# Gate loads in pieces and a different pace of gathers in a two-layer decoder trunk on one Trainium2 core

## The chip, the cores and the metric

The kernel runs on one core of one Trainium2 chip. The metric is the device time of one execution in microseconds (us); lower is better. Times given as "before" are the median of three timed runs, with the lowest and the highest. The profile is one further execution, with a time of its own. Engines are called as in the profile: PE (matrix engine), DVE (vector), ACT (scalar), POOL (GpSimd) and SP (which here only issues DMAs).

## What is computed

A decoder trunk of two layers for 512 tokens of width 1024, in float32. Each layer has a mixer (layer 1: gated linear attention and memory attention; layer 2: stick-breaking attention and memory attention), a layer norm, and then PEER: a feed-forward layer that picks, for each token and each of 8 heads, 16 of 16384 experts, and a second layer norm. Only PEER is touched by the change:

```python
def apply_experts(args):            # xt (128, D), it and gt (128, heads, 16): indices and gates
    xt, it, gt = args
    act = jax.nn.gelu(jnp.einsum('nd,nhkd->nhk', xt, u_tab[it]), approximate=False)
    return jnp.einsum('nhk,nhkd->nd', gt * act, v_tab[it])
...
h = layer_norm(DEEPNORM_ALPHA * h + mix, ln_g[layer, 0], ln_b[layer, 0])
ffn = peer(h, peer_w_q[layer], peer_subkeys[layer], peer_u[layer], peer_v[layer])
h = layer_norm(DEEPNORM_ALPHA * h + ffn, ln_g[layer, 1], ln_b[layer, 1])
```

## The kernel before, in words

`peer` runs twice (called "the first PEER" and "the second PEER" here). It treats the 512 tokens in two ways.

*Dense, for 384 tokens.* All 16384 experts are computed for these tokens, 128 experts at a time, in `P` = 128 blocks. A first pass, **u** (`ublock`), multiplies a block of `u_tab` with the tokens and keeps the gelu of it (`act`, written to `Ad` in DRAM, or `keep` in SBUF for the last 16 blocks). Each float32 operand is split in a high and a low part (`split`: `uh`, `ul` or `vh`, `vl`), and a product takes three matmuls: high by high, high by low, low by high (lines 117 to 119 in u, 289 to 293 and 1866 to 1868 in v). Meanwhile the top 16 of the scores are found, and turned into a dense table of gates, which goes to `Gd` in DRAM. A second pass, **v** (`vprep` and the loop behind it), reads the gates back (`gl`), multiplies them with the activations (`w`, line 1798), splits that (`whi` on ACT, line 1809, `wlo` on DVE, line 1810), and multiplies it with a block of `v_tab` into accumulators that stay in PSUM for the whole pass. v takes the 16 blocks in `keep` first (for the first 6 of them the gates lie in the tile named `keep` too), then the other 112. In v one block is 18 matmuls of 512 columns: 3 token tiles by two halves of the width by three.

*Gathered, for 128 tokens, and u of 32 more.* POOL fetches one expert row per token by an indirect DMA (`gather`, line 1167, a tile `gr` of 128x1024, `PF` = 3 ahead), and DVE takes a product with it: `gather_u` in a dot product with the tokens (a SCALAR_TENSOR_TENSOR at line 1109, written `gr<-gr,xnat`), `gather_v` in a sum (`va`, line 1246). A PEER has 160 gathers of u (128 and two times 16) and 128 of v, 288 together. They are put between the dense blocks by the `Stream` `gus`: each block hands it a budget in nanoseconds, each gather costs 1200 of it, and what is left is carried over. The budget is `GQ` in the query part ahead of u, `GU` in u while the selection (`work`) goes on, `GU2` after that up to block `KB` = 112, `GU3` for blocks 112 to 126, and in v `vb`, which is computed so that the gathers end `VE` blocks ahead of v's end. When the 128 gathers of v are done, `finish(0, ...)` takes the layer norm of their 128 tokens on DVE (`lny`, line 1022, to `xnat`, line 1039).

*Order.* In `peer` the order on PE, DVE, ACT and POOL is that of the code. In v, `vprep(b + 2)` stands ahead of the matmuls of block b, so a block is prepared two blocks before it is multiplied; the last `TAIL` = 6 blocks are prepared ahead and multiplied at the end, one token tile after another. The order on SP's queue is set by the framework's scheduler. The rows of `u_tab` and `v_tab` (512 KB a block, `ur` and `vr`, line 82) have `RB` = 4 buffers: the load of block i waits on SP until `vl` of block i-4 is done, and what stands behind it on SP waits too.

*Gate loads before.* v's gates come in nine loads: one for the first 6 blocks (into `keep`), one for the next 10 (tag `gx`), and seven for 16 blocks each (3072 KB, tags `big` and `xhl` by turns). The second and the third are issued on ACT's queue by `preload(1)` and `preload(2)`, the others on SP's by `vprep`, one DMA each. The activations `al` (352 KB for two blocks) are loaded on SP too.

```python
if b < P - 1:
    gus(GU if work.q else GU2 if b < KB else GU3)
...
vb = 1200 * (2 * P + SD - gcount[0] + PF) / (P - VE - VS)
```

Of the kernel before, what the change touches and what calls it, by code (L numbers as in the profile page):

```python
# [1066 lines left out]
NSUB = TD // TS  # L1067
AB = 2
AL = 2
GB = 16  # L1070
GA = 6
OT = 4
DT = 8
WB, WB0 = 900, 1850
GU = 1200
WP = 1100
LOG = 0
PF = 3
VS = 3
GD = 1  # L1080
G0 = 6
VE = 8
GU2 = 1850
GU3 = 1850
WF = 6100
ER = 6
GQ = 900
# [26 lines left out]
def peer(E, mixer, wq, sk, ut, vt, un, lng, lnb, out_dram=None, follow=()):  # L1114


    nc, tc = E.nc, E.tc
    Gd = E.dram.tile([NSUB, P, P, TS], F32, tag="Gd", name="Gd")
# [7 lines left out]
    with ExitStack() as pp:  # L1126
# [129 lines left out]
        with ExitStack() as up:  # L1256
# [449 lines left out]
            def ublock(b):  # L1706
# [28 lines left out]
                if b < P - 1:  # L1735
                    gus(GU if work.q else GU2 if b < KB else GU3)
                if LOG:
# [18 lines left out]
        gcuts = [0, G0] + list(range(KEEP, P + 1, GB))  # L1756
        vorder = list(range(KB, P)) + list(range(KB))

        def new_gates(i, i1):
            k = gcuts.index(i)  # L1760
            pool, tag = (wv, "gx") if k == 1 else (gp, "big") if k % 2 else (E.xp, "xhl")
            return pool.tile([P, NSUB, i1 - i, TS], F32, tag=tag, name="gl", bufs=1)

        def load_gates(eng, dst, b, b1):
            eng.dma_start(dst, Gd[:, :, b:b1].rearrange("s p i n -> p s i n"))

        pre = {}

        def preload(k, eng=nc.scalar):
            i, i1 = gcuts[k:k + 2]  # L1770
            pre[i] = new_gates(i, i1)
            load_gates(eng, pre[i], vorder[i], vorder[i] + i1 - i)

        def vprep(i):
            if i >= P:
                return
            b = vorder[i]
            raw = load_raw(E, vt[b * P:(b + 1) * P], "vr")
            if i + GA in gcuts[3:-1]:
                preload(gcuts.index(i + GA), nc.sync)  # L1780
            if i in gcuts:
                if i == 0:
                    vp["g"] = g0
                    load_gates(nc.sync, g0, b, b + G0)
                else:
                    vp["g"] = pre.pop(i)
                vp["i"] = i
            if b >= KB:
                av = keep[:, b - KB]
            else:  # L1790
                if b % AL == 0:
                    vp["a"] = wv.tile([P, AL, TU], F32, tag="al", name="al", bufs=3)
                    nc.sync.dma_start(vp["a"].rearrange("p (g a) n -> p g a n", a=AB), Ad[b // AB:b // AB + AL // AB].rearrange("g p a n -> p g a n"))
                av = vp["a"][:, b % AL]
            w = wv.tile([P, TD], F32, tag="w", name="w")
            whi = wv.tile([P, TD], F32R, tag="whi", name="whi", bufs=TAIL)
            wlo = wv.tile([P, TD], F32R, tag="wlo", name="wlo", bufs=TAIL)
            nc.vector.tensor_mul(w[:, :TU].rearrange("p (s n) -> p s n", n=TS), vp["g"][:, :TU // TS, i - vp["i"]],  # L1798
                                 av.rearrange("p (s n) -> p s n", n=TS))
            nc.scalar.activation(w[:, TU:].rearrange("p (s n) -> p s n", n=TS), vp["g"][:, TU // TS:, i - vp["i"]], AF.Copy)  # L1800
            pool, j = None, i - (P - TAIL)
            if j == 0:
                vp["tb"] = gp.tile([P, 16 * NT * P], F32R, tag="big", name="vtail")
            if 0 <= j < 4:
                pool = lambda name: vp["tb"][:, (2 * j + "hl".index(name[-1])) * D:][:, :D]
            elif j >= 4:
                pool = lambda name: gp.tile([P, D], F32R, tag="gr", name=name, bufs=PF + 1)
            hi, lo = split(E, raw, "v", pool)
            nc.scalar.activation(whi, w, AF.Copy)  # L1809
            nc.vector.tensor_sub(wlo, w, whi.bitcast(F32))  # L1810
            vp[i] = (whi, wlo, hi, lo)

        tail = []
        with written:
# [4 lines left out]
            acc = [[psum(E, name=f"acc{t}_{h}") for h in range(2)] for t in range(ND)]  # L1819
            vb = 1200 * (2 * P + SD - gcount[0] + PF) / (P - VE - VS)  # L1820

            preload(1)
            for b in range(P):
                vprep(b + 2)
                if b == 6:
                    preload(2)
                if b >= P - TAIL:
                    tail.append(vp.pop(b))
                    continue
                whi, wlo, hi, lo = vp.pop(b)  # L1830
                for t in range(ND):
                    sl = slice(t * P, (t + 1) * P)
                    mov_mm(E, acc[t], whi[:, sl], wlo[:, sl], hi, lo, b == 0, False)
                if b == P // 2:
                    vp["ln"] = load_ln(E, wv, lng, lnb)
                if b == P // 2 + 8:
                    warm_sqrt(E, vp["ln"][0])
                if b >= VS:
                    gus(vb)
# [14 lines left out]
            for t in range(ND):  # L1854
                sl = slice(t * P, (t + 1) * P)
# [4 lines left out]
                else:  # L1860
                    c = 0
                    for a in parts:
                        hs = slice(c, c + a.shape[-1])
                        c = hs.stop
# [99 lines left out]
```

## Time and profile before

| | |
|---|---|
| three timed runs | median 2860.54 us, lowest 2859.91, highest 2874.1 |
| the profiled execution | 2854.29 us, its span 2852.5 us |
| DVE busy | 2398.5 us (84%) |
| ACT busy | 1440.2 us (50%) |
| POOL busy | 969.8 us (34%) |
| moved by DMA | 821.25 MB, mean 288 GB/s |
| chain that ended last | PE 67%, DVE 12%, DMA 8%, issue 7%, POOL 4%, ACT 2% |
| the two dense passes, from the trace | u from 331 to 881 us and 1748 to 2299 us, v from 886 to about 1425 us and 2303 to about 2845 us |

The span goes from the first to the last instruction on the profile's clock; the profiled execution's own time is 1.8 us longer. A row of waits reads: engine, tile and line that waited, then `<-` what released it, then total us, number of times, and the longest one. A row of the timeline reads: start, duration, engine (with a q: its queue), line, operation, tiles out`<-`in, shapes, and in brackets the idle time before it with what ended that. A row of windows gives the stretch, its length, busy us of each engine with the instructions in it, the clock that TensorE was granted (1.00 is full), the busy share of the 16 DMA engines, and GB/s. GB/s rows of the DMA view divide their window into 40 equal slices.

### The profile page before, as it was taken

To read this page: it belongs to the slowest core of one execution; us is meant where nothing else is said; L and a number is where in the kernel's file an instruction comes from. 1 tells how busy PE (TensorE), PEld (TensorE's weight loads), DVE (VectorE), ACT (ScalarE), POOL (GpSimd) and SP (SyncE) were. 2 spreads that over 40 slices of the span, in tenths; PEclk is the share of its full clock that TensorE was granted. 3 is DMA by queue.
4 is the path that set the end of the run, shared out by engine and by line. 5 is a ranking of instruction groups with operands and counts; after the bars stand their busy time and mean duration, and the time that the engine had idled before them with its cause. 6 is when DMAs were issued, how large, how long until landed. Compare 5 with 4: busy or idle time off the path is not lost.

```text
span 2852.5 us, 44767 instructions
## 1 busy us (share of the span) xinstructions
PE 2806.3 (98%) x16235; PEld 2479.6 (87%) x16235; DVE 2398.5 (84%) x4806; ACT 1440.2 (50%) x2699; POOL 969.8 (34%) x675
## 2 busy tenths in 40 slices
PE   9999999999999999999999999999999999999998
PEld 8888999999998888788787889999999988887886
DVE  5565999999887888788968859999998878887888
ACT  6342447668683334333346434475786733333432
POOL 0102534343343344344100025344433524443440
PEclk9999999999999999999999999999999999999999
DMA  5332599999999999999621326999999999999994
GB/s 195 111 104 78 183 309 337 323 339 349 368 402 350 367 365 376 364 359 364 214 71 48 111 89 208 321 329 319 345 358 373 389 355 359 365 368 360 371 365 156
DMA packets 274701, 821.25 MB, mean 288 GB/s; under 512 B 34384, under 2 KB 83760, under 8 KB 268080
## 3 DMA queue, kind: packets, MB, share of 16 engines
q1 hardware_dynamic: 154880, 411.09, 40.6%
q0 software_dynamic: 82944, 302.03, 29.3%
q10 hardware_dynamic: 36656, 105.28, 9.6%
q8 instruction: 127, 2.08, 0.3%
q14 instruction: 94, 0.77, 0.1%
HBM read 723.31 MB, written 92.90 MB: 286 GB/s over the span
## 4 chain that ended last, share of the span: by engine, by line
PE 67%; DVE 12%; DMA 8%; issue 7%; POOL 4%; ACT 2%; ACTq 0%; POOLq 0%; DVEq 0%; SPq 0%
PE acc L291 9%; PE acc L289 9%; PE acc L293 9%; DMA vr<-in_vt 7%; PE ph L117 5%; PE ph L119 5%; PE ph L118 5%; POOL gr L1167 4%; DVE gr L1109 3%; PE pq L117 2%; PE pq L118 2%; PE pq L119 2%; DVE ul L1109 2%; PE bsp L117 1%; PE pss L1666 1%
## 5 line engine op out<-in xcount | busy, mean ns | idle before, releaser
L117 PE MATMUL ph<-xhl,uh 128*128 128x352 f32 x2048 | 674.6, 329 | 0.0
L119 PE MATMUL ph<-xhl,ul 128*128 128x352 f32 x2048 | 662.5, 323 | 5.6 <-DVE ul L1109 5.2
L118 PE MATMUL ph<-xhl,uh 128*128 128x352 f32 x2048 | 660.7, 323 | 0.0
L1167 POOL DMA_INDIRECT gr<-in_vt,gidx x256 | 376.7, 1471 | 526.4 <-DVE va L1246 465.6
L1167 POOL DMA_INDIRECT gr<-in_un,gidx x256 | 336.9, 1316 | 541.6 <-DVE gr L1109 446.8
L289 PE MATMUL acc<-vh,whi 128*128 128x512 f32 x1480 | 460.6, 393 | 22.2 <-ACT whi L1809 22.2
L97 ACT ACTIVATE vh<-vr 128x1024 fp32r<-128x1024 f32 x248 | 262.2, 1057 | 396.6 <-PE acc L293 270.7
L291 PE MATMUL acc<-vl,whi 128*128 128x512 f32 x1480 | 460.3, 392 | 1.0
L293 PE MATMUL acc<-vh,wlo 128*128 128x512 f32 x1480 | 458.5, 391 | 0.0
L98 DVE TENSOR_TENSOR vl<-vr,vh 128x1024 fp32r<-128x1024 f32 x248 | 303.1, 1222 | 165.2 <-ACT vh L97 164.8
L97 ACT ACTIVATE uh<-ur 128x1024 fp32r<-128x1024 f32 x288 | 303.8, 1055 | 227.1 <-PE ph L118 163.1
L119 PEld LDWEIGHTS ph<-xhl,ul 128*128 128x128 f32 x2048 | 385.1, 188 | 10.1 <-DVE ul L1109 8.7
L118 PEld LDWEIGHTS ph<-xhl,uh 128*128 128x128 f32 x2048 | 386.0, 188 | 0.0
L117 PEld LDWEIGHTS ph<-xhl,uh 128*128 128x128 f32 x2048 | 385.5, 188 | 0.1
L1109 DVE SCALAR_TENSOR_TENSOR gr<-gr,xnat 128x1024 f32<-128x1024 f32 x256 | 321.4, 1261 | 40.5 <-DMA gr<-in_un,gidx 40.5
L289 PEld LDWEIGHTS acc<-vh,whi 128*128 128x128 f32 x1480 | 278.5, 189 | 85.7 <-ACT whi L1809 28.3
L291 PEld LDWEIGHTS acc<-vl,whi 128*128 128x128 f32 x1480 | 278.5, 189 | 64.0 <-DVE vl L98 6.5
L293 PEld LDWEIGHTS acc<-vh,wlo 128*128 128x128 f32 x1480 | 279.0, 189 | 59.7 <-DVE wlo L1810 2.4
L1246 DVE SCALAR_TENSOR_TENSOR va<-gr,gw,va 128x1024 f32<-128x1024 f32 x254 | 325.1, 1280 | 1.4
L98 POOL TENSOR_TENSOR ul<-ur,uh 128x1024 fp32r<-128x1024 f32 x60 | 144.3, 2407 | 461.3 <-DVE s L1273 337.7
L1109 DVE TENSOR_TENSOR ul<-ur,uh 128x1024 fp32r<-128x1024 f32 x220 | 268.0, 1218 | 8.1 <-ACT uh L97 4.9
L1809 ACT ACTIVATE whi<-w 128x384 fp32r<-128x384 f32 x256 | 132.5, 518 | 218.4 <-DVE w L1798 218.0
(389 smaller groups left out, 4568.2 us busy)
## 6 DMA issues: line engine op xcount, KB each, us to landing
ur<-in_ut SPq DMA_DIRECT2D x256, 512.0 KB
vr<-in_vt SPq DMA_DIRECT2D x256, 512.0 KB
Gd<-gt ACTq DMA_DIRECT2D x48, 1024.0 KB
Ad<-act ACTq DMA_DIRECT2D x112, 352.0 KB
al<-Ad SPq DMA_DIRECT2D x112, 352.0 KB
gl<-Gd SPq DMA_DIRECT2D x12, 3072.0 KB
ur<-in_wq SPq DMA_DIRECT2D x32, 512.0 KB
bs<-in_b_st SPq DMA_DIRECT2D x14, 512.0 KB
```

The lines of the kernel that those rows point to most:

```text
L97: nc.scalar.activation(hi, raw, AF.Copy)
L98: sub = lambda eng=eng: eng.tensor_sub(lo, raw, hi.bitcast(F32))
L117: nc.tensor.matmul(ps, h, xhi[:, c, sl], start=(c == 0), stop=False)
L118: nc.tensor.matmul(ps, h, xlo[:, c, sl], start=False, stop=False)
L119: nc.tensor.matmul(ps, l, xhi[:, c, sl], start=False, stop=(c == NC - 1))
L289: nc.tensor.matmul(acc[hf], lh, hi[:, hf * 512:(hf + 1) * 512], start=first, stop=False)
L291: nc.tensor.matmul(acc[hf], lh, lo[:, hf * 512:(hf + 1) * 512], start=False, stop=False)
L293: nc.tensor.matmul(acc[hf], ll, hi[:, hf * 512:(hf + 1) * 512], start=False, stop=last)
L1109: self.ins = op(*args, **kw)
L1167: nc.gpsimd.indirect_dma_start(out=gr, out_offset=None, in_=tab, in_offset=bass.IndirectOffsetOnAxis(ap=idx[:, k:k + 1], axis=0))
L1246: nc.vector.scalar_tensor_tensor(va, gr, gw[:, k:k + 1], va, op0=ALU.mult, op1=ALU.add)
L1809: nc.scalar.activation(whi, w, AF.Copy)
```

## The change

The seven constants set how early and in how many pieces gates are loaded (`GA`, `GP`), and how the gathers are spread (`GU`, `GU2`, `GU3`, `VE`). A gate load becomes `GP` = 4 DMAs of 6 of the 24 groups of tokens each, one per block, all on SP's queue and each in the `vprep` of one block, from ten blocks ahead of the first use. The load for the first 6 blocks stays whole.

```diff
-GA = 6
+GA = 10
+GP = 4
-GU = 1200
+GU = 1250
-VE = 8
+VE = 9
-GU2 = 1850
-GU3 = 1850
+GU2 = 1700
+GU3 = 1400
-        def load_gates(eng, dst, b, b1):
-            eng.dma_start(dst, Gd[:, :, b:b1].rearrange("s p i n -> p s i n"))
+        def load_gates(dst, b, b1, sl=slice(None)):
+            nc.sync.dma_start(dst[:, sl], Gd[sl, :, b:b1].rearrange("s p i n -> p s i n"))
-        def preload(k, eng=nc.scalar):
-            i, i1 = gcuts[k:k + 2]
-            pre[i] = new_gates(i, i1)
-            load_gates(eng, pre[i], vorder[i], vorder[i] + i1 - i)
+        def preload(i):
+
+            for c, c1 in zip(gcuts[1:], gcuts[2:]):
+                q = i - max(1, c - GA)
+                if 0 <= q < GP:
+                    if q == 0:
+                        pre[c] = new_gates(c, c1)
+                    load_gates(pre[c], vorder[c], vorder[c] + c1 - c, slice(q * NSUB // GP, (q + 1) * NSUB // GP))
         def vprep(i):
             raw = load_raw(E, vt[b * P:(b + 1) * P], "vr")
-            if i + GA in gcuts[3:-1]:
-                preload(gcuts.index(i + GA), nc.sync)
+            preload(i)
-                    load_gates(nc.sync, g0, b, b + G0)
+                    load_gates(g0, b, b + G0)
-            preload(1)
             for b in range(P):
                 vprep(b + 2)
-                if b == 6:
-                    preload(2)
```

Line numbers grow by one behind the constants, and by three or four behind `preload`. Of the 288 gathers of a PEER, 152 are issued before v's first block in the old program and 147 in the new one; up to block 76 of u the new one gets ahead, by one gather each at blocks 4, 28, 52 and 76, and it falls behind from block 93 on.

**SP's queue, in v of the first PEER, where the gates for blocks 32 to 47 are loaded.** Before, one DMA of 24 groups stands ahead of four rows of `v_tab`:

```order
L82 DMA vr<-in_vt 128x1024 x15
L1765 DMA gl<-Gd 128x24x256
L82 DMA vr<-in_vt 128x1024 x4
L1793 DMA al<-Ad 128x704
L82 DMA vr<-in_vt 128x1024
L1793 DMA al<-Ad 128x704
```

Now, at the same row of `v_tab` (the 19th), the first of four pieces of 6 groups:

```order
L1766 DMA gl<-Gd 128x6x256
L82 DMA vr<-in_vt 128x1024
L1766 DMA gl<-Gd 128x6x256
L82 DMA vr<-in_vt 128x1024
L1797 DMA al<-Ad 128x704
L1766 DMA gl<-Gd 128x6x256
L82 DMA vr<-in_vt 128x1024
L1766 DMA gl<-Gd 128x6x256
L82 DMA vr<-in_vt 128x1024
```

The load begins at the same place, and a row of `v_tab` now has one piece ahead of it in place of the whole.

**DVE, where u ends and v begins, in the first PEER.** `ul` is the split of a u block, `gr,gh<-gr,xnat` a gather's product, `w<-keep` the first instruction of v. Before:

```order
L1109 TENSOR_TENSOR ul<-ur,uh 128x1024
L1109 SCALAR_TENSOR_TENSOR gr,gh<-gr,xnat 128x1024
L1109 TENSOR_TENSOR ul<-ur,uh 128x1024
L1109 SCALAR_TENSOR_TENSOR gr,gh<-gr,xnat 128x1024 x2
L1109 TENSOR_TENSOR ul<-ur,uh 128x1024
L1109 SCALAR_TENSOR_TENSOR gr,gh<-gr,xnat 128x1024 x3
L1798 TENSOR_TENSOR w<-keep 128x352
```

Now:

```order
L1110 TENSOR_TENSOR ul<-ur,uh 128x1024
L1110 SCALAR_TENSOR_TENSOR gr,gh<-gr,xnat 128x1024
L1110 TENSOR_TENSOR ul<-ur,uh 128x1024
L1110 SCALAR_TENSOR_TENSOR gr,gh<-gr,xnat 128x1024
L1110 TENSOR_TENSOR ul<-ur,uh 128x1024
L1110 SCALAR_TENSOR_TENSOR gr,gh<-gr,xnat 128x1024 x2
L1802 TENSOR_TENSOR w<-keep 128x352
```

Of the products between the third last `ul` and `w`, six before, four are left, and of the three behind the last `ul`, two. On ACT's queue the last write of `Gd` in u moves ahead by one block (five splits of u stand behind it in place of four), and on SP's queue the load of `keep` stands ahead of the last row of `u_tab` and no longer behind it.

**DVE, near the end of v, in the first PEER.** `va` is a gather's sum, `lny` begins the layer norm of the gathered tokens, `vtail` is `vl` of a block whose split is kept to the end. Before, from the split of block 121:

```order
L98 TENSOR_TENSOR vl<-vr,vh 128x1024
L1810 TENSOR_TENSOR wlo<-w,whi 128x384
L1246 SCALAR_TENSOR_TENSOR va<-gr,gw,va 128x1024
L1798 TENSOR_TENSOR w<-gl,al 128x352
L98 TENSOR_TENSOR vtail<-vr,vtail 128x1024
L1810 TENSOR_TENSOR wlo<-w,whi 128x384
L1246 SCALAR_TENSOR_TENSOR va<-gr,gw,va 128x1024
L1022 SCALAR_TENSOR_TENSOR lny<-xnat,va 128x512
```

Now, from the same block's `w`:

```order
L1247 SCALAR_TENSOR_TENSOR va<-gr,gw,va 128x1024
L1802 TENSOR_TENSOR w<-gl,al 128x352
L98 TENSOR_TENSOR vl<-vr,vh 128x1024
L1814 TENSOR_TENSOR wlo<-w,whi 128x384
L1022 SCALAR_TENSOR_TENSOR lny<-xnat,va 128x512
L1024 BN_STATS lnst<-lny 128x6
```

Two products that stood behind `wlo` of block 121 stand ahead of it now, and the layer norm ends ahead of block 122, where it ended ahead of block 123.

## Prediction

> **What bounds the kernel now.** I read the share of each engine first.
>
> ```profile
> PE 2806.3 (98%) x16235; PEld 2479.6 (87%) x16235; DVE 2398.5 (84%) x4806; ACT 1440.2 (50%) x2699; POOL 969.8 (34%) x675
> ```
>
> PE works for 98% of the span, so a change that takes no matmul away can only win back what PE waits. The waits of PE name two of any size:
>
> ```profile
> PE acc L289 <- ACT whi L1809: 26.0, 21, 4.8
> PE ph L119 <- DVE ul L1109: 5.2, 10, 0.8
> ```
>
> The first is all in v. The same view by stretch says where: in 900 to 1390 us and 2310 to 2810 us (inside v), at 870 to 900 and 2290 to 2310 (from u to v), and at 1390 to 1412 (the end of v; 2810 to 2830 gives the same row):
>
> ```profile
> PE acc L289 <- ACT whi L1809: 5.6, 4, 3.2
> PE acc L289 <- ACT whi L1809: 6.0, 5, 3.4
> PE acc L289 <- ACT whi L1809: 4.8, 1, 4.8
> PE acc L289 <- ACT whi L1809: 4.4, 1, 4.4
> PE acc L289 <- ACT whi L1809: 2.6, 5, 1.2
> ```
>
> A wait of PE can cost more than itself. Only four stretches of v or its start are granted half the clock, and each follows one of the four waits above 3 us; the waits of 1.2 us are followed by none:
>
> ```profile
> 884.80:891.60 6.80, 5.92 (x14) 4.71 (x15) 0.00 (x0) 0.50 1.03 404
> 1168.10:1171.50 3.40, 3.40 (x9) 2.59 (x8) 0.00 (x0) 0.50 0.90 311
> 2301.30:2308.10 6.80, 4.98 (x12) 3.92 (x13) 0.00 (x0) 0.50 1.03 406
> 2588.00:2591.40 3.40, 3.40 (x9) 2.63 (x10) 0.00 (x0) 0.51 0.77 290
> ```
>
> Half of PE's busy time there is lost: 2.96 and 2.49 us at v's start, 1.7 and 1.7 us inside v. So 41 us at most are to be had: 11.6 + 3.4 inside v, 9.2 + 5.5 at its start, 5.2 at its end, and about 6 us in u.
>
> **The change part by part. Gate loads.** The longest wait inside v, with what stands ahead of it:
>
> ```profile
> 1140.02 0.44 SPq L1765 DMA_DIRECT2D gl<-Gd  x1
> 1141.62 13.02 SPq L82 DMA_DIRECT2D vr<-in_vt  x4
> 1165.39 1.06 ACT L97 ACTIVATE vh<-vr 128x1024 fp32r<-128x1024 f32 x1 [12.29 <-DMA vr<-in_vt]
> 1166.91 0.74 PE L289 MATMUL acc<-vh,whi 128*128 128x512 f32 x2 [3.20 <-ACT whi L1809]
> ```
>
> The row of `v_tab` issued behind the 3072 KB of gates lands 23.8 us after its issue, and PE misses it by 3.2 us: its cushion is about 20.6 us. The other waits in this stretch likewise lie some 20 to 29 us behind a gate load. Now 768 KB stand ahead of that row in place of 3072. At the pace of this stretch (3584 KB in 23.8 us) 768 + 512 KB take 8.5 us, far inside the cushion. The fourth row behind the load is the dangerous one now, as all four pieces are ahead of it. But PE wants it three blocks of 4.1 us later than the first (12.2 us), and the bytes ahead of it are those that had left before: before, the load, this row and three more were in by 1169 us, as ACT split them one behind the other. So it comes some 5 us early. I take 14 of the 15.0 us (11.6 waits, 3.4 clock), and leave 1 for the load of the layer norm's vectors that falls into the longest wait. The bounds are nothing and 15.0.
>
> The pieces make 64 gate DMAs of 16. An issue occupies SP for 0.44 us in the row above, and SP mostly waits for free buffers, which hides it; if it did not, 48 x 0.44 = 21 us would be the price. The Trainium skill ("DMA: Bandwidth & Descriptors", section "Measured (HBM→SBUF, 128 partitions, SWDGE, issued from GpSimd)") speaks against pieces: DMAs should be batched to 1 MiB or more, for at least 75% of the peak rate. By that rule pieces of 768 KB would slow the loads; the trace does not bear it out, since v's other DMAs are all of 512 or 352 KB and the rate is best where these run alone (rows below).
>
> **v has to carry more.** Five gathers of 512 KB a PEER move from u to v. Rates of the DMA engines in 1076 to 1141 us (one gate load, at its start), in 40 slices:
>
> ```profile
> GB/s 394 382 355 349 370 385 393 381 368 378 393 408 403 408 404 401 287 368 144 355 373 328 396 412 395 403 391 383 391 401 381 281 360 300 373 416 415 389 419 368
> 950.00:1015.00 65.00, 65.00 (x288) 53.85 (x287) 55.55 (x68) 26.15 (x48) 26.92 (x19) 1.00 1.00 377
> ```
>
> The mean is 373, slices reach 400 to 419, and a few fall to 144 or 287, where the queues had caught up. So the engines could carry some 400. Five gathers over 110 blocks are 0.045 a block, 24 KB or 6 GB/s more: under that. DVE has 9.5 us idle in 65 in the second row, against 0.045 x 16 x 1.28 = 0.9 us. Cost nothing; if there were no room in the DMA engines, ten gathers of 0.524 MB at 373 GB/s would cost 14 us.
>
> **From u to v.** DVE and ACT at this place, in the first PEER:
>
> ```profile
> 874.45 1.22 DVE L1109 TENSOR_TENSOR ul<-ur,uh 128x1024 fp32r<-128x1024 f32 x1
> 876.93 1.23 DVE L1109 SCALAR_TENSOR_TENSOR gr<-gr,xnat 128x1024 f32<-128x1024 f32 x1 [1.26 <-DMA gr<-in_un,gidx]
> 880.78 1.23 DVE L1109 SCALAR_TENSOR_TENSOR gr<-gr,xnat 128x1024 f32<-128x1024 f32 x1 [2.62 <-DMA gr<-in_un,gidx]
> 883.36 1.22 DVE L1109 SCALAR_TENSOR_TENSOR gr<-gr,xnat 128x1024 f32<-128x1024 f32 x1 [1.34 <-DMA gr<-in_un,gidx]
> 884.51 0.52 DVE L1798 TENSOR_TENSOR w<-keep 128x352 f32<-128x352 f32 x1
> 876.63 0.23 ACT L1800 ACTIVATE w<-keep 128x32 f32<-128x32 f32 x1 [2.94 <-DMA keep<-Gd]
> 878.66 1.06 ACT L97 ACTIVATE vh<-vr 128x1024 fp32r<-128x1024 f32 x1 [1.80 <-DMA vr<-in_vt]
> 885.11 0.52 ACT L1809 ACTIVATE whi<-w 128x384 fp32r<-128x384 f32 x1 [5.39 <-DVE w L1798]
> ```
>
> PE ends u at 880.9. v's gates and its first row of `v_tab` were there by 876.6 and 878.7; what came last is `w`, since DVE stood in order behind three products whose gathers came late: u asked for six gathers in its last three blocks. Now it asks for four, two of them behind the last `ul`. Each is then issued some 10 us ahead of its use instead of 6.5, so I expect them landed: 875.7 + 2 x 1.23 = 878.1, then `w`, and `whi` behind `vh` at 878.66 + 1.06 + 0.5 = 880.2. That is just in time. The load of `keep` also leaves a block earlier. What is late next is `vr`: 1 to 2 us would then remain as a wait, too short for the clock to fall. Both waits and both clock dips are 14.7 us; I take 13. Bounds nothing and 14.7.
>
> **The end of v.** DVE in the first PEER, from `wlo` of block 121 to that of block 127, with nothing idle between:
>
> ```profile
> 1386.80 0.55 DVE L1810 TENSOR_TENSOR wlo<-w,whi 128x384 fp32r<-128x384 f32 x1
> 1387.27 1.28 DVE L1246 SCALAR_TENSOR_TENSOR va<-gr,gw,va 128x1024 f32<-128x1024 f32 x1
> 1390.51 1.28 DVE L1246 SCALAR_TENSOR_TENSOR va<-gr,gw,va 128x1024 f32<-128x1024 f32 x1
> 1398.18 0.52 DVE L1798 TENSOR_TENSOR w<-gl,al 128x352 f32<-128x352 f32 x1
> 1407.92 0.55 DVE L1810 TENSOR_TENSOR wlo<-w,whi 128x384 fp32r<-128x384 f32 x1
> ```
>
> The two `va` products leave this stretch, so the last `wlo` comes 2 x 1.28 = 2.56 us sooner, about the 2.6 us that PE waits here. Ahead of block 121 DVE idles some 0.7 us a block, which covers them. 5 us for both PEERs; bounds nothing and 5.2.
>
> **u gets more to do.** In u up to block 85 DVE is as full as PE, and less so behind:
>
> ```profile
> 560.00:640.00 80.00, 79.79 (x587) 77.42 (x586) 79.04 (x257) 52.29 (x114) 42.21 (x24) 1.00 0.93 330
> 780.00:860.00 80.00, 80.00 (x619) 77.70 (x618) 71.96 (x93) 63.10 (x149) 38.62 (x27) 1.00 1.01 402
> 364.56 1.22 DVE L1109 SCALAR_TENSOR_TENSOR gr<-gr,xnat 128x1024 f32<-128x1024 f32 x1
> PE ph L119 <- DVE ul L1109: 2.7, 5, 0.8
> PE ph L119 <- DVE ul L1109: 2.5, 5, 0.8
> ```
>
> (The last two rows: waits in the u of the first and of the second PEER.) A product more, 1.23 us with its accumulator read, reaches PE wherever `ul` is just in time. In the first u PE waits at 378 to 395, at 552 and at 640 us. The extra product at block 4 (346 us) stands ahead of the first of these, those at blocks 28 (442) and 52 (547) ahead of the next, the one at block 76 (654) behind all. So three of four reach PE: 2 x 3 x 1.23 = +7.4 us. Bounds: nothing, if the little idle time of DVE takes them up, and twice that, since pieces of the selection move by a block too and may meet a tight spot.
>
> **Sum:** -14 - 13 - 5 + 7.4 = -24.6 us. The profiled execution took 2854.29 us, its span and 1.8 us around it; that gives 2829.7. The median of the timed runs is 6.25 us above that execution, so I predict 2836 us.
>
> **The rivals.**
>
> *v's start waits on.* `vr` or `keep` is late and not the gathers, since the first pieces of gates now mix with these rows on SP's queue. For it: ACT waited for both (2.94 and 1.80 us). Against: both were there 2 us ahead of PE's need. The 13 us stay: 2849.
>
> *The pieces wait as the whole did.* The bytes are the same and the fourth row comes too late. The 14 us stay: 2850. Against it stands the 5 us margin above.
>
> *u takes twice as much* (15 us): 2844.
>
> *Slower: v is at the end of its DMA engines.* Their busy share is 1.00 in the row from 950 us. If 373 to 377 GB/s is all they give, ten more gathers lengthen v by 14 us, the backlog behind each gate load is not worked off before the next, so the 14 us inside v stay, and the 13 at its start too, where the same engines carry gates, rows and gathers: 2836 + 14 + 14 + 13 = 2877. It decides once v asks for more than they give, 373 + 6 GB/s; slices of 400 to 419 speak against it.
>
> *Each DMA costs its issue*, unhidden: 2836 + 21 = 2857. [...]
>
> **How the numbers follow.** About 0.5% (14 us) is what a measurement of this kernel can tell from no change. The forecast has 0.70, v's start 0.12, the pieces 0.05, the doubled u 0.06, the full DMA engines 0.05, the issues 0.02. Faster by over 0.5% means under 2846: the forecast and half of the doubled u, 0.73. Slower by over 0.5% (above 2875): the full DMA engines, 0.05. The rest is 0.22. Low end: all waits gone and u for nothing, 15.0 + 14.7 + 5.2 = 35 us, 2826, less 3 for the spread of the timed runs. High end: the two rivals at 2849 and 2850, plus 3. 2823 to 2853 leaves out 0.07 and some tails.
>
> **What would show it.** Right: no wait of `vh` for `vr` of 12 us in v, no clock row of 0.50 at 1168, 2588, 885 and 2301 us, PE's wait at line 289 from 26.0 us to under 5, and its wait at line 119 from 5.2 to about 12. Wrong: a wait of DVE for a gather or of ACT for `vr` at v's start, or waits in v that recur every 65 us.

## The result, and the profile after

The changed kernel takes 2825.65 us (median of 4 runs, 2822.52 to 2827.53) against 2864.51 us (4 runs, 2859.91 to 2874.1) of the kernel before: a ratio of 0.9859 with a 95% interval of 0.9828 to 0.989, so 1.4% less. Its profiled execution took 2827.47 us with a span of 2825.8 us (before: 2854.29 and 2852.5). The medians lie 38.9 us apart, the two profiled spans 26.7 us, since the profiled execution of the kernel before was one of its shortest; what follows accounts for the 26.7 us.

The engine row and the waits of PE over the whole span (the columns as in the part on time and profile above; L1110, L1598 and L1813 are the changed kernel's lines for what were 1109, 1597 and 1809):

```profile
PE 2797.6 (99%) x16235; PEld 2479.0 (88%) x16235; DVE 2399.3 (85%) x4806; ACT 1443.7 (51%) x2699; POOL 952.1 (34%) x675
```

```profile
PE ph L119 <- DVE ul L1110: 7.0, 12, 0.9
PE pg L1598 <- ACT obl L1578: 6.0, 4, 3.7
PE acc L289 <- ACT whi L1813: 1.4, 4, 0.3
```

The wait at line 289 fell from 26.0 to 1.4 us. What is left of it stands at the two ends of v, where this row of the waits in 1365 to 1400 us is the same for the second PEER (2770 to 2815):

```profile
PE acc L289 <- ACT whi L1813: 0.7, 2, 0.3
```

Inside v and at its start the same view lists no wait of PE at all. Inside v it was close, though. In the second PEER, where the gates for blocks 80 to 95 are loaded, the third and the fourth piece with the row of `v_tab` behind each, and then ACT's split of the first of these two rows and PE's first matmul with it:

```profile
2549.20 0.88 SPq L1766 DMA_DIRECT2D gl<-Gd  x1
2550.80 2.65 SPq L82 DMA_DIRECT2D vr<-in_vt  x1
2553.50 0.99 SPq L1766 DMA_DIRECT2D gl<-Gd  x1
2557.11 8.11 SPq L82 DMA_DIRECT2D vr<-in_vt  x1
2571.22 1.06 ACT L97 ACTIVATE vh<-vr 128x1024 fp32r<-128x1024 f32 x1 [8.93 <-DMA vr<-in_vt]
2572.75 0.73 PE L289 MATMUL acc<-vh,whi 128*128 128x512 f32 x2
```

The row issued at 2550.80 us is split 20.4 us later, and PE begins 1.53 us after that. Before the change, where PE had waited for the split (1165.39 us), it began 1.52 us behind it (1166.91). So here the row came with nothing to spare; in the first PEER it had 1.8 us.

At v's start (timeline of the first PEER) another thing comes last now:

```profile
880.02 1.06 ACT L97 ACTIVATE uh<-ur 128x1024 fp32r<-128x1024 f32 x1 [5.40 <-DMA ur<-in_ut]
884.55 0.52 DVE L1802 TENSOR_TENSOR w<-keep 128x352 f32<-128x352 f32 x1
888.54 0.63 PE L289 MATMUL acc<-vh,whi 128*128 128x512 f32 x2
```

The gathers are there in time; the last row of `u_tab` is what ACT waits for. But `w` begins 4 us before PE wants it, so that nothing is lost.

The row at `PE pg` has grown (0.6 us before). Most of it is one long wait in each PEER, in u at 520 and 1924 us. The timeline around the first, SP's queue and then ACT and PE:

```profile
502.04 10.18 SPq L1159 DMA_DIRECT2D xr<-xnat  x8
512.42 0.67 SPq L82 DMA_DIRECT2D ur<-in_ut  x1
520.68 1.06 ACT L97 ACTIVATE uh<-ur 128x1024 fp32r<-128x1024 f32 x1 [4.62 <-DMA ur<-in_ut]
523.95 0.23 PE L1598 MATMUL pg<-ob,obl 128*128 128x128 f16 x1 [3.65 <-ACT obl L1578]
```

`xr` are the rows of 16 tokens for which u is gathered too (the "side group"); eight small loads bring them, and on SP they stand ahead of a row of `u_tab`. In the kernel before they took less long, one row later, and PE did not wait:

```profile
504.28 6.90 SPq L1158 DMA_DIRECT2D xr<-xnat  x8
```

Now PE has to wait, and after each of the two waits the clock is halved for 3.4 us. The windows of the changed kernel, with two stretches of v behind them:

```profile
525.20:528.60 3.40, 3.40 (x14) 3.40 (x13) 1.79 (x7) 3.40 (x10) 0.15 (x1) 0.50 0.99 380
1928.10:1931.50 3.40, 3.40 (x14) 3.40 (x13) 3.18 (x10) 3.40 (x10) 0.95 (x1) 0.50 0.95 370
1080.00:1145.00 65.00, 65.00 (x289) 53.81 (x288) 57.45 (x69) 26.32 (x48) 26.38 (x20) 1.00 1.02 383
1145.00:1210.00 65.00, 65.00 (x289) 53.81 (x288) 57.27 (x69) 27.82 (x50) 29.25 (x20) 1.00 1.02 391
```

The last two stretches before the change:

```profile
1080.00:1145.00 65.00, 64.99 (x287) 53.38 (x287) 55.48 (x68) 25.69 (x48) 30.17 (x19) 1.00 1.01 372
1145.00:1210.00 65.00, 61.69 (x264) 50.25 (x263) 51.38 (x63) 24.72 (x46) 24.48 (x18) 0.97 1.00 367
```

PE is full in v now, and the DMA engines move 383 and 391 GB/s where they moved 372 and 367. The length of each stage, from the starts of its first and last matmul in the trace (us; first and second PEER, u, the gap from u to v, v up to its last six blocks, and these):

| kernel | u | gap | v | last blocks | span |
|---|---|---|---|---|---|
| before | 549.5, 550.1 | 5.1, 4.7 | 510.9, 511.6 | 30.4, 28.6 | 2852.5 |
| changed | 557.2, 555.4 | 0.2, 0.2 | 497.8, 499.4 | 27.9, 26.1 | 2825.8 |
| pieces alone | 549.0, 551.0 | 4.6, 3.4 | 499.5, 500.5 | 30.4, 28.6 | 2828.5 |
| gathers alone | 554.4, 557.5 | 0.2, 0.1 | 520.4, 523.1 | 27.9, 26.1 | 2871.5 |
| one piece | 556.3, 555.9 | 0.1, 0.2 | 512.6, 518.5 | 27.8, 26.1 | 2859.0 |
| budget 1200 | 550.2, 549.3 | 0.2, 0.1 | 500.0, 499.4 | 29.2, 27.4 | 2817.5 |
| budget 1150 | 549.7, 549.8 | 0.3, 2.0 | 509.7, 513.0 | 26.0, 24.3 | 2836.5 |

By the first two rows the span fell by 26.7 us: 9.4 of the gaps, 25.3 of v and 5.0 of the last blocks, less 13.0 that u takes more. The last five rows belong to the experiments that follow.

### The profile page after: what moved, and what is told of

It is laid out like the page before. It is cut to its first block, busy times and chain, and to the rows that moved or that the text cites. A ratio compares the mean times of both kernels' runs of the same rounds, so it can differ in the third digit from the quotient of the medians.

```text
span 2825.8 us, 44841 instructions
## 1 busy us (share of the span) xinstructions
PE 2797.6 (99%) x16235; PEld 2479.0 (88%) x16235; DVE 2399.3 (85%) x4806; ACT 1443.7 (51%) x2699; POOL 952.1 (34%) x675
## 3 DMA queue, kind: packets, MB, share of 16 engines
q0 software_dynamic: 82944, 302.03, 29.2%
## 4 chain that ended last, share of the span: by engine, by line
PE 82%; DVE 12%; DMA 3%; issue 1%; ACT 1%; SPq 0%; ACTq 0%; POOL 0%; DVEq 0%
PE acc L291 11%; PE acc L289 11%; PE acc L293 11%; PE ph L117 8%; PE ph L119 8%; PE ph L118 8%; DVE gr L1110 3%; PE pq L117 2%; PE pq L118 2%; PE pq L119 2%; DVE ul L1110 2%; DMA vr<-in_vt 1%; DVE ob L1110 1%; PE pg L1598 1%; PE pg L1597 1%
## 5 line engine op out<-in xcount | busy, mean ns | idle before, releaser
L1168 POOL DMA_INDIRECT gr<-in_vt,gidx x256 | 355.8, 1390 | 484.6 <-DVE va L1247 423.8
L1110 DVE SCALAR_TENSOR_TENSOR gr<-gr,xnat 128x1024 f32<-128x1024 f32 x256 | 321.2, 1263 | 9.8 <-DMA gr<-in_un,gidx 9.7
L1110 DVE TENSOR_TENSOR ul<-ur,uh 128x1024 fp32r<-128x1024 f32 x220 | 268.3, 1219 | 33.1 <-ACT uh L97 26.0
L1578 ACT ACTIVATE obl<-ob,rat 128x128 f16<-128x128 f16 x704 | 224.9, 394 | 38.0 <-DVE ob L1110 20.4
```

Of the source, the lines that this page charges most:

```text
L1110: self.ins = op(*args, **kw)
L1168: nc.gpsimd.indirect_dma_start(out=gr, out_offset=None, in_=tab, in_offset=bass.IndirectOffsetOnAxis(ap=idx[:, k:k + 1], axis=0))
L1578: nc.scalar.activation(obl[:, q], ob[:, q, 0], AF.Copy, scale=rat[:, n0 + q:n0 + q + 1])
```

## The experiments

The changed kernel's edit has two halves. The first two runs do one each.

### The pieces alone

```diff
-GU = 1250
+GU = 1200
-VE = 9
-GU2 = 1700
-GU3 = 1400
+VE = 8
+GU2 = 1850
+GU3 = 1850
```

> The gate pieces alone: all three budgets of u's gathers and the number of va products left for the end of v are as before the change. Theory (the two halves act apart): the waits of PE at line 289 inside v and their two stretches of half clock go (15.0 us before), and some 5 us more of short pauses with them; the waits at v's start (4.8 and 4.4 us) with their half clock stay, since DVE still stands behind three products there; the end of v stays (2.6 us each); u is as before. About 15 to 20 us shorter than before: a profiled span of 2832 to 2838 us. Rival A (the rows of v's start come earlier because the second gate load no longer lies on ACT's queue): v's start is mended too, another 15 us, about 2820. Rival B (the room made by fewer gathers in v's start is what lets the pieces land): waits inside v remain, over 2845.

Measured: 2830.02 us (2829.54 to 2832.45), a ratio to before of 0.9898 (0.9876 to 0.992), span 2828.5. Waits of PE, then of DVE, in 850 to 905 us:

```profile
PE acc L289 <- ACT whi L1813: 4.4, 1, 4.4
```

```profile
DVE gr L1110 <- DMA gr<-in_un,gidx: 12.6, 8, 3.2
```

Inside v the waits are down to 1.9 us in both PEERs, the longest 1.2, with no half clock; at its start PE still waits 4.4 us, with DVE waiting for gathers. The theory holds (the span is even 3.5 us under its range): the pieces mend v, and not its start. Most of the change's gain is here.

### The gathers alone

The edit is to the kernel before:

```diff
-GU = 1200
+GU = 1250
-VE = 8
-GU2 = 1850
-GU3 = 1850
+VE = 9
+GU2 = 1700
+GU3 = 1400
```

> The new budgets of the gathers alone, with whole gate loads, six blocks ahead, as before the change. Theory: v's start is mended (9.4 us of gaps and 5.5 us of half clock), the end of v is 5 us shorter, u is 13 us longer as in the changed kernel, and the gate waits inside v stay (15 us or, with five more gathers a pass in v, a few us more). Sum about 2 to 7 us shorter than before, a span of 2845 to 2851 us: a change that could hardly be measured by itself. Rival (v's start needs the pieces, since the whole gate loads hold its rows back): the start keeps its waits and the kernel is 8 us longer than before, about 2860.

Measured: 2869.29 us (10 runs, 2862.61 to 2875.72), ratio 1.0018 (1.0001 to 1.0034), span 2871.5. Neither theory had it: v's start and end are mended as the first said (gap 0.2, last blocks 27.9 and 26.1), but v itself grew by 9.5 and 11.5 us. Windows inside v:

```profile
950.00:1015.00 65.00, 62.37 (x267) 50.71 (x267) 54.78 (x68) 25.33 (x48) 27.80 (x20) 0.97 0.97 358
1015.00:1080.00 65.00, 63.73 (x280) 52.10 (x279) 55.15 (x67) 24.52 (x47) 27.21 (x20) 1.00 0.99 365
1080.00:1145.00 65.00, 62.03 (x265) 50.63 (x265) 52.80 (x64) 24.27 (x45) 28.05 (x19) 0.97 0.98 359
1145.00:1210.00 65.00, 60.50 (x259) 49.32 (x258) 51.00 (x61) 24.55 (x45) 25.46 (x18) 0.97 0.98 364
```

PE is short in all four, and the DMA engines move only 358 to 365 GB/s. With whole gate loads v had no room for five more gathers a PEER, some 2 us each by these two profiles. They lie at opposite ends of their kernels' times, so part of this is the spread between executions: the gaps, the half clock at v's start, the last blocks and u alone would make the kernel 7.6 us shorter, and the medians say 5.4 longer, which leaves about 13 us for v, 1.3 a gather. With pieces v has the room (the changed kernel's v is as long as that of the pieces alone, within 0.6 us, but for the half clock at the latter's start). So the halves don't add: 5 us lost by the one (its interval begins at a ratio of 1.0001), 34 won by the other (medians), and 39 by both.

### One piece, as early as the pieces

```diff
-GP = 4
+GP = 1
```

> The changed kernel with each gate load in one piece of 3072 KB, still ten blocks ahead of its use and on SP's queue. Theory (the size of a piece does it, since the row behind it lands only when the whole piece has): the waits of PE at line 289 inside v come back, once a group of 16 blocks, 1 to 3 us each with short pauses beside them, 15 to 25 us in all: a span of 2841 to 2851 us. Rival (the four blocks of earlier start do it): no wait comes back, within 2 us of the changed kernel's 2825.8.

Measured: 2862.65 us (10 runs, 2855.4 to 2868.25), ratio 1.0002 (0.9987 to 1.0016), span 2859.0. PE's waits over the span, and how long a row of `v_tab` takes from issue to landing in 900 to 1390 us (shortest, median, longest):

```profile
PE acc L289 <- ACT whi L1813: 21.8, 14, 4.4
```

```profile
DMA to landing us min/median/max: 4.4/6.9/23.1
```

The waits are back and the whole gain with them, more than expected. Four blocks of an earlier start are worth nothing.

### Four pieces, begun six blocks ahead

```diff
-GA = 10
+GA = 6
```

> The changed kernel with the four pieces begun six blocks ahead of their use in place of ten, so that the last piece is asked for three blocks (some 12 us) ahead; pieces and budgets stay. Theory (it is the size of a piece that decides, and a piece of 768 KB lands within 9 us): no wait of over 0.5 us in v, within 2 us of the changed kernel, 2824 to 2828. Rival (the earlier start is needed too): ACT or DVE waits for gl at each group of 16 blocks and PE with it, 1 to 3 us seven times a pass, 2835 to 2860.

Measured: 2824.65 us (2824.15 to 2825.53), span 2823.8: the same as the changed kernel. The landing of a row of `v_tab` in the same stretch:

```profile
DMA to landing us min/median/max: 3.4/7.2/18.5
```

The view lists no wait of PE inside v. With the run before, this settles that the size of the piece does it. This view knows the landing of only some of the rows; the next section compares them all with the cushion of 20.6 us that the prediction read from the trace. The pieces themselves took 7.6 to 20.5 us to land in this stretch, half of them over 13.6 us, and not the 9 us of the expectation.

### Two pieces

```diff
-GP = 4
+GP = 2
```

> The changed kernel with each gate load in two pieces of 1536 KB in place of four of 768. Theory (the row behind a piece lands when the piece and it have gone through the DMA engines, and PE misses it once that takes longer than the row's cushion, about 20.6 us by the trace of before): at the pace of that place, 3584 KB in 23.8 us, 1536 + 512 KB take 13.6 us, so no wait above 0.5 us in v, and the time is within 3 us of the changed kernel's, 2823 to 2829. Rival (any longer piece costs in proportion): half of what the whole load costs, 15 to 18 us, about 2842.

Measured: 2830.55 us (2828.98 to 2830.9), beside the changed kernel's 2826.88 (2825.45 to 2828.72) on the same chip. v is 502.5 and 500.6 us long, 4.7 and 1.2 more than in the changed kernel's profile, and nearly all of the 4.7 is lost at one place (timeline):

```profile
1150.66 0.34 ACTq L1051 DMA_DIRECT2D gam<-in_lng  x1
1151.04 0.45 ACTq L1052 DMA_DIRECT2D bet<-in_lnb  x1
1170.63 1.06 ACT L97 ACTIVATE vh<-vr 128x1024 fp32r<-128x1024 f32 x1 [11.80 <-DMA vr<-in_vt]
1172.15 1.22 PE L289 MATMUL acc<-vh,whi 128*128 128x512 f32 x2 [2.90 <-ACT whi L1813]
```

The layer norm's vectors are loaded on ACT's queue just behind a half of a gate load, and PE waits 2.9 us, with half clock behind it (1.7 us). The estimate of 13.6 us was too short: this row took 23.5 us, with these other loads in between.

The trace of each kernel also gives, for every row that ACT stood waiting for, the time from its issue on SP to its split on ACT, and the wait of PE at its block. The three longest in v, both PEERs together:

| kernel | issue to split, us | PE's wait, us |
|---|---|---|
| before | 24.0, 23.8, 22.0 | 3.4, 3.2, 1.4 |
| one piece | 25.0, 24.3, 23.2 | 4.4, 3.7, 2.6 |
| two pieces | 23.5, 22.2, 18.8 | 2.9, 1.7, none |
| four pieces (changed) | 20.4, 18.6, 18.2 | none |

Each wait is what exceeds the cushion of 20.6 us, to within 0.1 us. So the waits inside v come from rows that land later than their cushion, in all four kernels, and the cost falls far faster than the size: some 36 us with one piece (2862.65 against 2826.88), 4 with two, none that can be seen with four.

### The last blocks of u

```diff
-GU3 = 1400
+GU3 = 1850
```

> The changed kernel with the third budget (u's blocks from 112 on) back at 1850, so that DVE again has two products ahead of the last ul and three behind it, as in the kernel before; pieces, ten blocks and the other budgets stay. Theory (v's start waited for products of gathers that are asked for too late and too close together): PE waits 3 to 5 us at each of v's two starts, each with 3.4 us of half clock (1.7 us lost), some 10 to 13 us in all, and the end of v stays as in the changed kernel: a span of about 2836 us. Rival (the waits went because the gate loads no longer hold up the rows and keep): no wait there, 2824 to 2826 us.

Measured: 2840.61 us (2836.28 to 2841.28), span 2834.6. The size is about as expected, the form only in part (of the 8.8 us of span, 3.0 are the two gaps). Waits of ACT in 850 to 905 us, and of PE in 2275 to 2320 us:

```profile
ACT uh L97 <- DMA ur<-in_ut: 9.3, 1, 9.3
```

```profile
PE ph L117 <- ACT uh L97: 2.2, 1, 2.2
```

The waits at v's start return (gaps of 2.4 and 1.0 us), but with the row of `u_tab` ahead of them late as well, and with one stretch of half clock (at 890.4 us) instead of two. So the pace of the gathers in u's last blocks is what mended v's start. That gathers close together hold back the other loads of that place too is argued from these two rows, no more.

### The small loads on another queue

```diff
-nc.sync.dma_start(xr[h * TS:(h + 1) * TS], E.x[S0 + g * TS:S0 + (g + 1) * TS, ST])
+nc.scalar.dma_start(xr[h * TS:(h + 1) * TS], E.x[S0 + g * TS:S0 + (g + 1) * TS, ST])
```

> The changed kernel with the eight small loads of the side group's rows (xr) issued from ACT's queue instead of SP's; nothing else. Theory (in the changed kernel the second group's eight loads hold SP for 10 us ahead of a row of u's table, so that ACT, then PE wait 3.65 and 1.77 us for it at 520 and 1924 us, each followed by 3.4 us of half clock): both waits and both stretches of half clock go, 3.65 + 1.77 + 2 x 1.7 = 8.8 us: a span of about 2817 us. Rival A (DVE's extra products are what makes these rows late, since they hold the raw buffers): the waits stay, 2825. Rival B (ACT then pays for the issues): waits of PE for ACT appear elsewhere, 2822 to 2828.

Measured: 2841.92 us (2838.67 to 2843.79), span 2838.6: 16 us worse by the medians, 13 by the spans. My theory falls: freeing SP of them does not help. Rival B had the kind of it, but not the size. ACT and its queue at the place:

```profile
507.16 11.55 ACTq L1159 DMA_DIRECT2D xr<-xnat  x5
518.76 1.06 ACT L97 ACTIVATE uh<-ur 128x1024 fp32r<-128x1024 f32 x1 [11.86 <-DMA ur<-in_ut]
521.52 0.29 PE L1598 MATMUL pg<-ob,obl 128*128 128x128 f16 x1 [6.85 <-ACT obl L1578]
```

The bracket puts ACT's wait down to a row of `u_tab`, but by the trace (rows and splits counted in order) the row that this `uh` splits was issued at 493.90 and had landed at 500.28 us. What ACT stood behind is the issue of the last five small loads, which come ahead of `uh` in its program. Of the 11.55 us the issues themselves take 2.7. The rest is waiting: the DMAs of the program share a few completion semaphores, and the last three loads begin at 509.88, 514.89 and 518.20 us, each 0.02 us after the landing of the DMA that used its semaphore before (a store of `Gd` and two rows of `u_tab`). So ACT, and PE 6.85 us with it, waited for landings that it had no need of yet.

### Fewer gathers in u

Four runs change `GU` alone (the one with 1150 ends the `va` products a block sooner too). By the end of u the changed kernel has asked for 147 gathers, with 1240, 1220, 1200 and 1150 it is 146, 145, 144 and 140 (before: 152). The expectation for 1200 overstates this; three fewer is right.

```diff
-GU = 1250
+GU = 1200
```

> The changed kernel with the first budget of u's gathers back at 1200 (the places of the gathers in the first 80 blocks of u are as before, so 8 to 9 fewer a PEER lie in u than in the changed kernel). Theory (the +13 us of u are DVE's extra products and the side group's loads that meet them): u is back at 549.5 to 550.5 us a PEER, the wait of PE pg for ACT obl and the half clock at 525 and 1928 us are gone, and v keeps its gain: a span of 2811 to 2816 us. Rival A (v then carries eight gathers a PEER more and is at the limit of its DMA engines, 1.4 us each): v takes 22 us back, about 2830 or more. Rival B (u's loss comes from something else, such as the gate or keep loads): u stays at 555 to 557 us, about 2826.

Measured: 2819.56 us (2817.43 to 2820.0), ratio to before 0.9858 (0.9836 to 0.988), span 2817.5, just above the range. The wait at `pg` and the half clock of 525 and 1928 us are gone, u is back at 550.2 and 549.3 us, and v grew by 2.2 us in the first PEER only. The last blocks take 1.3 us more in each (one `va` product comes later).

```diff
-GU = 1250
-VE = 9
+GU = 1150
+VE = 10
```

> The changed kernel with the first budget of u at 1150, below that of the kernel before (four products a PEER less before v than with 1200, seven less than in the changed kernel), and with va's products ended a block sooner (VE = 10). Theory (in u each product of DVE near its limit costs its 1.23 us, and v has room for the gathers): u takes 545 to 548 us a PEER, v 498 to 500, its end 27.9 and 26.1 as in the changed kernel: a span of 2806 to 2813 us. Rival A (v is at the end of its DMA engines): waits for vr come in v and it takes 505 to 510 us, 2820 to 2830. Rival B (the rest of u's waits has another cause): u stays at 550, 2815 to 2817.

Measured: 2834.1 us (2830.15 to 2838.3), span 2836.5. u gains nothing more, and the first rival holds in v:

```profile
1080.00:1145.00 65.00, 63.87 (x279) 51.63 (x278) 55.15 (x66) 23.98 (x46) 29.39 (x20) 1.00 0.99 373
1145.00:1210.00 65.00, 62.45 (x267) 50.07 (x266) 53.15 (x63) 25.28 (x47) 26.79 (x20) 0.97 1.00 376
```

Beside the changed kernel's rows of the same stretches (383 and 391 GB/s, PE full) one sees that the DMA engines are nearly as busy (0.99 and 1.00 against 1.02), move less, and PE runs short. v is 25.5 us longer over both PEERs; less 5.1 for three stretches of half clock, that is 1.5 us for each of the 14 gathers. The room in v that the pieces made ends between 144 and 140 gathers before it (part of this may be the one block less that `VE` = 10 leaves).

```diff
-GU = 1250
+GU = 1220
```

> The changed kernel with the first budget of u's gathers at 1220: two gathers fewer than in the changed kernel by the end of u, and the second side group's eight small loads stand behind 63 rows of u's table (207 in the second PEER) as in the kernel before, no longer behind 62 (206); the end of u and of v keep the order of the changed kernel. Theory (those loads ahead of a row that is needed are what made the wait of 3.65 and 1.77 us with its half clock, and v has room for two gathers): u 550 to 552 us a PEER, v 498 to 500, its end 27.9 and 26.1: a span of 2813 to 2818 us. Rival A (the extra products alone do it): the waits stay, 2823 to 2826. Rival B (v is at the end of its DMA engines, as with budget 1150): v 503 to 506, about 2825.

```diff
-GU = 1250
+GU = 1240
```

> The changed kernel with the first budget at 1240: one gather fewer by block 60 and at the end of u than in the changed kernel, one more than with 1220, and the second side group's small loads still stand behind 62 rows (206). It differs from the kernel with 1220 in one gather by block 40 and in that place. Theory (the place of the small loads decides): the wait of PE pg for ACT obl stays, 1.8 to 3.7 us twice, each with 3.4 us of half clock, a span of 2822 to 2826 us. Rival (the number of products decides): about halfway between, 2818 to 2822, with waits half as long and no half clock.

The fourth has no edit:

> The changed kernel itself once more, beside the others on one chip, for the comparison with the budget of 1220: 2822 to 2828 us as measured before.

Measured on one chip: 2819.32 us with 1220 (5 runs, 2815.69 to 2825.06), 2820.74 with 1240 (4 runs, 2816.43 to 2823.86), 2826.88 for the changed kernel (4 runs, 2825.45 to 2828.72). Spans of the profiled ones: 2823.2, 2816.8, 2827.0. With 1240 the eight loads have the changed kernel's place on SP, yet (queue of SP; waits of PE in 490 to 545 us):

```profile
501.03 8.92 SPq L1159 DMA_DIRECT2D xr<-xnat  x8
510.04 0.53 SPq L82 DMA_DIRECT2D ur<-in_ut  x1
```

```profile
PE pg L1598 <- ACT obl L1578: 0.6, 1, 0.6
```

They take 8.9 us instead of 10.2, and the long wait isn't there; the median fits the rival. So their place does not decide, as I had thought. With 1220 they stand where they stood before, and another spot gives way (timeline and window of that kernel; this profiled execution, 2824.91 us, was among the longest of its five):

```profile
634.79 1.22 DVE L1110 SCALAR_TENSOR_TENSOR gr<-gr,xnat 128x1024 f32<-128x1024 f32 x1
637.56 1.22 DVE L1110 SCALAR_TENSOR_TENSOR gr<-gr,xnat 128x1024 f32<-128x1024 f32 x1
642.67 1.22 DVE L1110 TENSOR_TENSOR ul<-ur,uh 128x1024 fp32r<-128x1024 f32 x1
643.94 0.43 PE L119 MATMUL ph<-xhl,ul 128*128 128x352 f32 x1 [1.96 <-DVE ul L1110]
```

```profile
645.20:648.60 3.40, 3.40 (x13) 3.40 (x12) 3.37 (x5) 0.00 (x0) 2.70 (x2) 0.50 0.95 339
```

There two products fall ahead of one `ul`, with small pieces of the selection between and behind them (not shown) that fill DVE. So each budget beyond 1200 has its own meeting in u, with a price of 2 to 8 us a PEER that goes by no simple count: 2.1 to 4.5 us at 145 and 146 gathers, 5.3 to 7.7 at 147 in the changed kernel and its repetition, and 3.5 and 6.6 with the same 147 and two pieces.

## Why the prediction was right, and where it was off

**The time.** 2836 us were predicted and 2825.65 measured, within the range and near its low end. The four steps (pieces, gathers at v's start, end of v, u) each moved the way that was said. That their sum came so close is partly luck: u cost 5.6 us more than said, and 4.8 us that no term had, with 1.0 and 1.9 more than was taken at two others, made up for it. Of the 10.35 us, only 2.2 come from the sum of the terms (2829.7 us predicted for a profiled execution, 2827.47 found). 6.25 come from the step "The median of the timed runs is 6.25 us above that execution", which I carried over to the changed kernel; and 1.8 from the changed kernel's median lying below its own profiled execution. That step failed: the distance was no property of the kernel that stays. Beside these experiments the kernel before ran from 2854.82 to 2873.35 us (19 runs), so its profiled execution was one of the shortest. The two other kernels with whole gate loads spread over 13 us as well (gathers alone, one piece; 10 runs each); the changed kernel spread over 5.0 and 3.3 us in its two series of 4. It looks as if with the waits much of the spread went, and with it the distance; but the series differ in length, the budget of 1220 still spread over 9.4 us, and no run tests it.

**Gate waits: -14 predicted.** Gone, both waits and clock stretches, for the reason given: one piece brings them back, and the start four blocks earlier is no part of it. v fell by 25.3 us (13.1 + 12.2): 15.0 of these waits and their clock, 5.5 of the half clock at its start, and 4.8 that the rows of waits don't name. I did not break these down. The margin failed. The row behind the first piece was to land in 8.5 us, "far inside the cushion", and the fourth row "some 5 us early". When the changed kernel ran again, the rows behind the four pieces landed 13.5, 15.2, 19.6 and 18.2 us after their issue in the same place of the first PEER. So the third row is as late as the fourth; in the profile after the change the third had 1.8 and 0.0 us to spare in the two PEERs, the fourth 1.2 and 0.9. The estimate had left out that the pieces come faster than they can be moved: while they are issued, SP asks for 4 x 1280 KB and 704 KB of activations in four blocks of 4.08 us, 365 GB/s, and the gathers for some 160 more, against 391 that were moved at best (an estimate from these rows). That no wait was left in this profile is in part luck. The 48 more issues on SP showed nowhere as a wait of PE. The 1 us kept for the layer norm's vectors was not needed with four pieces; with two, the row that lands behind them was 2.9 us late, with half the clock after it.

**The rate with smaller DMAs.** In 1080 to 1145 us, where PE is full both times, the engines moved 383 GB/s with pieces and 372 before. In 1145 to 1210 us it was 391 with pieces, 367 before and 364 with whole loads and the new gathers. The rule of the Trainium skill ("DMA: Bandwidth & Descriptors", section "Measured (HBM→SBUF, 128 partitions, SWDGE, issued from GpSimd)") to batch DMAs to 1 MiB or more would have had v slower with pieces of 768 KB; the runs do not agree in this place.

**v carries more: nothing predicted.** Right for this kernel, and only beside the pieces. The room is small: the slower rival, that "v is at the end of its DMA engines", came true for v (not for its start) in the run of the gathers alone, and again with a budget of 1150, where it costs 1.5 us a gather (1.4 by the rival). The reading that the engines "could carry some 400", from single slices of 400 to 419, was too generous: no 65 us of v in any row above moved more than 391.

**From u to v: -13 predicted.** The gaps fell by 9.4 us and the 5.5 us of half clock went, 14.9 in all. The gathers were the cause, as the runs with the old third budget show. What was said to come last then (`vr`, 1 to 2 us late) did not; the last row of `u_tab` did, at no cost.

**The end of v: -5 predicted.** 30.4 to 27.9 and 28.6 to 26.1: 5.0.

**u gets more to do: +7.4 predicted, +13.0 measured** (557.2 - 549.5 and 555.4 - 550.1). This is the term that was mis-sized, and it went another way than was said. The extra products were to reach PE through `ul`, with the waits at line 119 going from 5.2 to about 12 us; they went to 7.0. The waits of 3.65 and 1.77 us at `pg` with 1.7 us of half clock each make 8.8 of it, which leaves some 4.2 for the extra products by themselves, less than was said. I had seen the 8.8 only as a bound ("may meet a tight spot"). The runs with 1200, 1220 and 1240 show that it is a meeting and no toll on each product. Why the eight loads take 10.2 us there and 6.9 before is left open. Over all profiles they took 8.6 to 11.2 us on SP where they stand behind 62 rows (206 in the second PEER) and 6.7 to 7.4 behind 63 (207); but with one gather less in u, at the first of these places, they took 8.9 and cost next to nothing.

**A version that is faster than both.** With 1200, 1220 and 1240 the medians are 6 to 7.6 us under the changed kernel's. That is 0.2 to 0.3%, less than the 0.5% that the prediction took as the bound; but no run with 1220 or 1240 was as long as the shortest of the changed kernel on that chip (2825.06 at most, against 2825.45).

## What to carry to other kernels

A transfer that is long beside the cushion of what stands behind it in a queue that several share should be cut until every row behind a piece lands within that cushion, and the rows behind the last pieces are the ones to look at, since the backlog has grown by then; starting it earlier does not do the same. Two edits that use the same engine's room should be tried one by one and together: here one of them loses alone (some 5 us) about what it wins beside the other (4). And the distance between a profiled execution and the median need not stay when the kernel changes, so a prediction should not carry it over without a range.

## What the runs showed of the hardware

*The granted clock.* The prediction had the clock at half only behind waits of PE above 3 us, and held 1 to 2 us for too short. The changed kernel's second wait at `pg`, and the same wait when the changed kernel ran again, with the window behind the latter:

```profile
1926.22 0.23 PE L1598 MATMUL pg<-ob,obl 128*128 128x128 f16 x1 [1.77 <-ACT obl L1578]
```

```profile
1927.65 0.23 PE L1598 MATMUL pg<-ob,obl 128*128 128x128 f16 x1 [1.57 <-ACT obl L1578]
```

```profile
1929.40:1932.80 3.40, 3.40 (x14) 3.40 (x13) 3.18 (x12) 3.40 (x10) 0.94 (x1) 0.50 1.02 403
```

Waits of 1.57, 1.77 and 1.96 us (the last with budget 1220) were followed by 3.4 us of half clock, which began 1.3 to 1.9 us after PE had gone on; the wait of 2.2 us quoted for the run on u's last blocks was not. So a wait's length alone does not decide between 1.6 and 2.2 us.

The trace shows what goes with it. In each profile the stretches of half clock begin on one grid of 3.413 us (525.2 and 1928.1 us are 411.0 steps apart). Count PE's idle time by the windows of that grid, in u and v of all fourteen profiles here. From full clock, every fall came right after a window in which PE idled 0.44 of it or more. No window with more than 0.54 was without one, and between the two there are both (35 falls in all). So 1.57 us that lay in one window were enough (0.46), and the 2.2 us were not, since they began at 2291.79 us and lay over two windows, in which PE idled 0.45 and 0.39.

*Small loads.* Eight loads of 16 rows took 6.7 to 11.2 us of SP's queue (with a busy share of the DMA engines of 0.93 after the change and 1.00 before, in the stretches shown). From ACT's queue they took 15.1 us, of which 8.8 are waits for the landings of other DMAs on the same semaphores, and they held up ACT itself.

*Rates.* With the engines' busy share at 0.97 to 1.02, they moved from 358 to 391 GB/s in 65 us of v, in kernels that differ in the pieces and in the number of gathers. A busy share of 1.00 is no sign of the best rate.
